# A two-layer decoder step on one core: convolution rows, weight transfers and small loads of the mixer put in another order

## The chip, the cores and the metric

The kernel runs on one core of a Trainium2 chip. TensorE (PE) does the matmuls, VectorE (DVE) and ScalarE (ACT) the elementwise work, GpSimd (POOL) small elementwise work and the issue of some transfers, SyncE (SP) the issue of all others. The metric is the device time of one execution in microseconds; less is better.

## What is computed

Two layers over 288 tokens (256 of a prompt, 8 sequences of 4), 2048 features wide. The mixer, the first half of a layer, is where the change lies:

```python
z = x @ w_in                          # u | cv | cg, 1024 columns each
y5, h_re, h_im = _s5(u, ...)          # 64 groups, complex scan over positions
g5 = gelu(y5)
s5_out = g5 * sigmoid(g5 @ s5_w_glu)
c = cv * sigmoid(cg)
c, new_conv = _causal_dwconv(c, conv_buf, conv_w, conv_b)   # 31 taps, per channel
c = silu(_ln(c, conv_ln_g, conv_ln_b))
x = _ln(ALPHA * x + concatenate([s5_out, c]) @ w_out, ln1_g, ln1_b)
...                                   # up, 3 taps, SwiGLU, down, LayerNorm
x = _ln(ALPHA * x + sigmoid(x @ pe_w_gate) * (p @ pe_w), ln3_g, ln3_b)
```

The output also holds the last scan states and the convolution inputs `new_conv`.

## The kernel before

Activations lie with features on the 128 partitions and the 288 tokens in the free direction. All weights stream once, in 128x128 blocks, eight blocks (512 KB) to a transfer (`wraw`). ScalarE rounds a transfer's tile to a high part (`whi`), VectorE subtracts to get the low part (`wlo`), and a block costs three matmuls of 288 columns (`run`, lines 372 to 378). The first ten transfers of the program are multiplied unsplit (line 368).

Nothing is scheduled by a tool: the program writes every engine's instructions in the order in which Python emits them. `run` walks the blocks of a phase and adds an estimate of TensorE's time to `pe_t`; every second block calls `tick`, which lets background generators emit pieces of other work. Generators wait with `wait(ns)` and `at(ns, fn)` on that account, so its entries (369 ns a block, 640 ns a convolution step) decide beside which block an instruction stands.

A mixer has these phases: `u0` (64 blocks, the first four tiles of u); eight phases `p0` to `p7` of 32 blocks, each giving the 128 channels of one convolution tile, with four phases `v1` to `v4` of 16 blocks between them (the other tiles of u); `g` (64 blocks, the half-GLU's weights); `o` (256 blocks, the output projection).

Two strands run beside these phases:

* **The scan**, eight steps c. TensorE multiplies u into the state (`inject`, tile `bu`, from `ust` and `em`), VectorE scans, and TensorE multiplies back (`project`, tile `y`, from `tm`, `hin` and `om`). `ust`, `tm` and, in layer 1, the parts of `em` and `om` (`sbt`, `sqb`, `scc`) are loaded by SyncE's queue; GpSimd copies into `hin`, makes the tables `stb` for ScalarE's sine and the decay rows `sd`, and stores `u_d`, `k_d` and `y_d` to memory, from where SyncE loads them in another layout. In layer 2 the tiles come ready from memory (`se_d`, `so_d`, `sk_d`, made during layer 1's FFN by `s5_early`).
* **The convolution**, eight tiles j. GpSimd loads the cached rows into `cbuf` (one buffer), VectorE writes the gated values in, GpSimd stores `cbuf` to memory (`cb_d`), loads the taps `cw` (one buffer), loads `cb_d` four times shifted into `stack` (one buffer, 1.1 MB in four transfers) and stores `cbuf` to the output. `conv(j)` then is eight steps of eight matmuls groups on TensorE (lines 1190 and 1193).

`conv(j - 1)` stands behind phase `p{j}`, and `stack(j)` behind that:

```python
self.run(ph[f"p{j}"], self.xs, ev)
if j:
    conv(j - 1)
while "done" not in part:
    self.late.pop(0)[1]()
stack(j)
```

`conv(6)` closes phase `p7`; `conv(7)` stands behind the first 32 blocks of `g`. A LayerNorm (`ln_finish`) is a chain of thirteen short VectorE instructions on 96x3 numbers between matmuls; at the end of layer 1 nothing else is there for TensorE in that time.

Of the kernel before, what the change touches and what calls it, by code (L numbers as in the profile page):

```python
# [65 lines left out]
LOOK = 1  # L66
EARLY_LAG = 7000.0
# [60 lines left out]
class Meter:  # L128
# [27 lines left out]
class Core:  # L156
    def __init__(self, tc, a, ctx):
        self.tc, self.nc, self.a, self.ctx = tc, tc.nc, a, ctx
        self.V = Meter(self, tc.nc.vector)
        self.pe_t = self.pe_l = self.dve_t = 0.0  # L160
# [185 lines left out]
    def run(self, blocks, xs, evac, sums=None, wide=False):  # L346
# [4 lines left out]
        for _, k, m in blocks:  # L351
# [17 lines left out]
            else:  # L369
                xh, xl = xs(k)  # L370
                self.pe_t += 369.0
# [35 lines left out]
    def ln_acc(self, st, v, last=False):  # L407
# [4 lines left out]
        if i == 0:  # L412
            def mean():
                cps = self.ln_banks(st, 1)[0]
                nc.tensor.matmul(cps[:, :TOK], self.ones_1, v, start=True, stop=True)
                st["c"], st["s1"], st["s2"] = self.ln_tile("ln_c"), self.ln_tile("ln_s1"), self.ln_tile("ln_s2")
                nc.scalar.activation(st["c"], cps[:, :TOK], AF.Copy, scale=1.0 / P)
# [31 lines left out]
    def ln_finish(self, st, fill=None, keep=False, subs=()):  # L449
# [26 lines left out]
        def sub(n=1):  # L476
            while subs and n:
# [30 lines left out]
        dg = self.lp.tile([TG, 3, TG], F32, tag="ln_dg", name="ln_dg", bufs=1)  # L508
        V.scalar_tensor_tensor(dg, self.ident[:TG, :TG].rearrange("p (o t) -> p o t", o=1).to_broadcast([TG, 3, TG]),
                               -1.0, y.rearrange("p (z o) -> p z o", o=1).to_broadcast([TG, 3, TG]),  # L510
                               op0=OP.mult, op1=OP.mult)
        fill(1)
        nc.tensor.matmul(b0[:, 8:8 + TOK], self.ones_1[:TG], dg.rearrange("p z t -> p (z t)"),
# [209 lines left out]
    def stack_tile(self, mp):  # L723
# [124 lines left out]
    def s5(self, l, mp):  # L848
# [56 lines left out]

        def load_o(c, eng):
            if early:
                o = mp.tile([P, 4, 2, 4, CIN], F32, name="sqb", tag="sqb", bufs=1)
                eng.dma_start(o, early[c][1])
                return (o,)  # L910
# [19 lines left out]
        def make_o(c, cc, bc=None):  # L930

            if early:
                kd, pk = early[c][2], cc
# [21 lines left out]
            kw = kd.rearrange("(q c) w -> c q w", q=4)  # L955

            def back():
                for s in range(4):
                    nc.sync.dma_start(tm[32 * s:32 * s + 32], kw[:, :, (3 - s) * 32:(3 - s) * 32 + P])
                self.at(LOAD_LAG, lambda: state.update(o=c))  # L960
            self.at(2000.0 if early else BACK_LAG, back)
# [60 lines left out]
        def project(c, us):  # L1022
            y = self.ps.tile([P, 512], F32, tag="one", name="y", bufs=1)
            self.pe_t += 1500.0
            for q in range(4):
                o = y[:, q * NCH:(q + 1) * NCH]
                self.strips(o, tm[:, q], us[:, q], True, False)
# [27 lines left out]
        early = self.early  # L1055
        state = {"i": -1, "p": -1, "e": -1, "o": -1, "y": False, "k": False}
# [64 lines left out]
        nxt = []  # L1121
        G.memset(bs, 0.0)
        G.memset(kp[:, 0:3], 0.0)
        G.memset(H[:, :, :, 0:1], 0.0)
        go0 = load_o(0, nc.gpsimd)
        bt0 = None if early else self.s5_load(l, 0, mp, nc.gpsimd, "b")
# [9 lines left out]
    def mixer(self, l, ph):  # L1136
        nc, a = self.nc, self.a
        V = self.V
        with self.tc.tile_pool(name="mx", bufs=1) as mp:
# [13 lines left out]
            stacks, cbuf = {}, {}  # L1153
# [449 lines left out]
```

## Time and profile before

| | |
|---|---|
| median of three runs | 2781.55 us (2775.46 to 2785.64) |
| the profiled execution | 2775.95 us |
| its span, first to last instruction | 2774.2 us |
| mean granted TensorE clock over the span | 0.985 of full |
| instructions | 57927 |
| bytes moved by DMA | 496.12 MB |

The span is what the trace covers; 1.75 us of the execution lie outside it. The clock is the share of 2.4 GHz that TensorE was granted; it has two levels here, 1.2 and 2.4 GHz, so 0.985 is a mean over stretches at either.

### The profile page before, as it was taken

The page shows a single profiled execution, that of the slowest core. Times are in us where ns is not written, and L with a number is a line of the kernel's source. Part 1 is how long each engine was busy: PE and PEld are TensorE (multiplying, and loading weights), DVE is VectorE, ACT ScalarE, POOL GpSimd, SP SyncE. Part 2 cuts the span into 40 slices and gives each one's busy share as a digit, 9 for nine tenths or more (in the row PEclk, how much of TensorE's full clock was granted, in tenths as well). Part 3 has the DMA queues.
Part 4 walks back from the last instruction along what each step waited for, and adds up shares of the span by engine and source line. Part 5 has one row for each costly group of instructions (what it writes and reads, how often), then busy time and mean ns, then how long its engine had stood idle before and what let it go on. Part 6 is the DMA issues. An engine that isn't in the chain of part 4 may idle for free.

```text
span 2774.2 us, 57927 instructions
## 1 busy us (share of the span) xinstructions
PE 2681.2 (97%) x23696; PEld 2622.5 (95%) x23696; DVE 1814.2 (65%) x3017; ACT 1351.3 (49%) x2224; POOL 299.8 (11%) x912
## 2 busy tenths in 40 slices
PE   8889999999999999999987999999999999999997
PEld 7878999999999999999986989999999999999997
DVE  5875768666577556667776548676546664566686
ACT  3444547553455345546453535465434553455363
POOL 3433001000010000000024410010000000000000
PEclk9999999999999999999998999999999999999998
DMA  7887545456556654554457875445554555455542
GB/s 240 240 234 223 174 155 171 149 174 204 183 183 193 207 172 155 172 174 152 161 184 217 244 219 169 151 160 163 180 168 152 170 182 162 156 172 167 167 153 102
DMA packets 188809, 496.12 MB, mean 179 GB/s; under 512 B 46368, under 2 KB 72240, under 8 KB 188544
## 3 DMA queue, kind: packets, MB, share of 16 engines
q1 hardware_dynamic: 174592, 444.00, 49.9%
q0 software_dynamic: 13952, 48.42, 6.2%
q8 instruction: 186, 3.05, 0.5%
q14 instruction: 79, 0.65, 0.1%
HBM read 467.47 MB, written 24.87 MB: 177 GB/s over the span
## 4 chain that ended last, share of the span: by engine, by line
PE 82%; DMA 8%; DVE 5%; issue 2%; ACT 1%; SPq 1%; POOL 1%; ACTq 0%; DVEq 0%; POOLq 0%
PE acc L372 26%; PE acc L378 24%; PE acc L377 24%; DMA out_dram<-cbuf 2%; PE acc L354 2%; PE acc L374 2%; DVE sw L142 1%; DVE wlo L142 1%; DMA cbuf<-in_convi_dram 1%; PE acc L368 1%; DMA wraw<-in_wts_dram 1%; DMA cb_d<-cbuf 1%; PE acc L1190 1%; DMA scc<-in_s5c_dram 1%; DMA sqb<-q_d 1%
## 5 line engine op out<-in xcount | busy, mean ns | idle before, releaser
L372 PE MATMUL acc<-xh,whi 128*128 128x288 f32 x4656 | 1388.7, 298 | 8.2 <-ACT e L1302 3.1
L377 PE MATMUL acc<-xl,whi 128*128 128x288 f32 x4357 | 1289.1, 296 | 0.4
L378 PE MATMUL acc<-xh,wlo 128*128 128x288 f32 x4357 | 1284.4, 295 | 0.4 <-issue 0.4
L142 DVE TENSOR_TENSOR wlo<-wraw,whi 128x1024 fp32r<-128x1024 f32 x766 | 923.4, 1228 | 47.4 <-ACT whi L198 32.8
L198 ACT ACTIVATE whi<-wraw 128x1024 fp32r<-128x1024 f32 x766 | 791.3, 1050 | 321.5 <-PE acc L377 186.6
L372 PEld LDWEIGHTS acc<-xh,whi 128*128 128x128 f32 x4656 | 876.7, 188 | 14.7 <-ACT e L1302 4.1
L377 PEld LDWEIGHTS acc<-xl,whi 128*128 128x128 f32 x4357 | 821.5, 189 | 3.2 <-DVE xl L142 1.3
L378 PEld LDWEIGHTS acc<-xh,wlo 128*128 128x128 f32 x4357 | 823.5, 189 | 0.9 <-issue 0.9
L372 PE MATMUL acc<-hh,whi 128*128 128x288 f32 x1408 | 416.8, 296 | 0.0
L142 DVE SCALAR_TENSOR_TENSOR fo<-fe,parf,fo 128x304 f32<-128x304 f32 x352 | 188.3, 535 | 332.6 <-ACT fo L1335 326.3
L377 PE MATMUL acc<-hl,whi 128*128 128x288 f32 x1312 | 387.8, 296 | 0.0
L378 PE MATMUL acc<-hh,wlo 128*128 128x288 f32 x1312 | 387.5, 295 | 0.0
L372 PEld LDWEIGHTS acc<-hh,whi 128*128 128x128 f32 x1408 | 264.9, 188 | 0.5
L378 PEld LDWEIGHTS acc<-hh,wlo 128*128 128x128 f32 x1312 | 247.2, 188 | 0.0
L377 PEld LDWEIGHTS acc<-hl,whi 128*128 128x128 f32 x1312 | 246.9, 188 | 0.0
L1331 ACT ACTIVATE fe<-acc 128x256 f32<-128x256 f32 x176 | 67.5, 384 | 299.7 <-PE acc L378 299.6
L1341 POOL COPY fstage<-fe 128x9 f32<-128x9 f32 x176 | 43.6, 248 | 1033.6 <-ACT fe L1332 1016.9
L431 ACT ACTIVATE ln_q<-x 128x288 f32<-128x288 f32 x90 | 40.2, 446 | 220.4 <-DVE x L142 220.4
L1335 ACT ACTIVATE fo<-fe,parf 128x304 f32<-128x304 f32 x176 | 112.9, 642 | 17.3 <-ACT fe L1332 1.1
L1355 ACT ACTIVATE hh<-fth 128x288 fp32r<-128x288 f32 x88 | 39.2, 445 | 164.4 <-DVE fth L142 164.4
L142 DVE TENSOR_TENSOR x<-x,acc 128x288 f32<-128x288 f32 x64 | 29.0, 454 | 131.5 <-PE acc L378 131.4
L142 DVE SCALAR_TENSOR_TENSOR x<-x,acc 128x288 f32<-128x288 f32 x64 | 28.9, 452 | 120.7 <-PE acc L378 120.5
(244 smaller groups left out, 2355.0 us busy)
## 6 DMA issues: line engine op xcount, KB each, us to landing
wraw<-in_wts_dram SPq DMA_DIRECT2D x776, 512.0 KB
stack<-cb_d POOLq DMA_DIRECT2D x56, 282.0 KB, 8.8
cw<-in_convw_dram POOLq DMA_DIRECT2D x16, 512.0 KB, 5.3
cbuf<-in_convi_dram POOLq DMA_DIRECT2D x16, 283.5 KB, 5.2
cb_d<-cbuf POOLq DMA_DIRECT2D x16, 283.5 KB, 3.7
out_dram<-cbuf POOLq DMA_DIRECT2D x16, 283.5 KB, 10.3
sbt<-in_s5b_dram SPq DMA_DIRECT2D x15, 256.0 KB
sqb<-q_d SPq DMA_DIRECT2D x60, 64.0 KB
```

The lines of the kernel that those rows point to most:

```text
L142: return f(out, *args, **kw)
L198: self.nc.scalar.activation(hi, self.raw[s], AF.Copy)
L354: nc.tensor.matmul(out, w, xl, start=False, stop=False)
L372: nc.tensor.matmul(out, w[0], xh, start=first, stop=False)
L374: nc.tensor.matmul(out, w[1], xh, start=False, stop=False)
L377: nc.tensor.matmul(out, w[0], xl, start=False, stop=False)
L378: nc.tensor.matmul(out, w[1], xh, start=False, stop=last)
L431: nc.scalar.activation(st["q"], v, AF.Square)
L1331: nc.scalar.activation(e[:, 2:2 + SEQ], acc[:, :SEQ], AF.Copy)
L1335: nc.scalar.activation(o[:, :w], e[:, 2:EW], AF.Identity, bias=self.prm("ffn_conv_b", m), scale=self.prm("ffn_conv_w2", m))
L1341: nc.gpsimd.tensor_copy(stage[:, z, :, 0], e[:, SEQ:EW:6])
L1355: nc.scalar.activation(hh[i], h, AF.Copy, scale=0.5)
```

## The change

1. **Output of the convolution rows.** `convo` is stored from `cb_d` in memory instead of from `cbuf`.
2. **Stack tiles.** Odd j use a second tile `big`, which later holds `phi` and `plo` (they had tiles of their own). `conv(j - 2)` instead of `conv(j - 1)` stands behind `p{j}`; the taps are loaded by themselves (`taps`), behind the convolution that frees `cw`. `conv(6)` moves into `g`, behind block 20; 12 blocks stand between it and `conv(7)`.
3. **Weight transfers.** The transfer that reuses a `wraw` tile was written into SyncE's queue right behind the subtraction that frees the tile. Now an account of VectorE's time (`dve_c`) says when the subtraction should be done, and the transfer is written 500 ns of `pe_t` behind that, or when the next eight blocks begin.
4. **Two tm tiles** in layer 2 (`pw` is the second); the load stands with that of `sqb`, a step earlier.
5. **GpSimd held at layer 2.** A one-column copy that reads `x32[0]` stands ahead of GpSimd's first work of the layer.
6. **Account.** A block counts 400 ns instead of 369, a convolution step 500 instead of 640. `ones_1` and `ln_dg` go, their room is shared with other tiles.

```diff
@@ stream_lo / next_block / tick
-            self.stream_dma(s + RAW_BUFS)
+            self.freed.append((s + RAW_BUFS, self.dve_c + FREE_LAG))
...
             self.stream_lo(s + ahead)
+            self.stream_dma(s + ahead + RAW_BUFS - 1)
...
+        while self.freed and self.freed[0][1] <= self.pe_t:
+            self.stream_dma(self.freed.pop(0)[0])
@@ Meter
+            cost = 150.0 + (2.1 if name == "tensor_tensor_scan" else 1.05) * n
+            self.core.dve_c = max(self.core.dve_c, self.core.pe_t) + cost
@@ run
-                self.pe_t += 369.0
+                self.pe_t += 400.0
@@ stack_tile
+        if j % 2:
+            return self.big_tile().bitcast(F32).rearrange("p (s w) -> p s w", s=4)
@@ s5
+        def load_t(c, kd):
+            t = tms[c % 2]
...
+        if l:
+            G.tensor_copy(kp[:, 0, 0, 0:1], self.x32[0][:, 0:1])
         G.memset(bs, 0.0)
@@ mixer
+            def taps(j):
+                cws[j] = mp.tile([P, 4, 8, 32], F32, tag="cw", name="cw", bufs=1)
+                nc.gpsimd.dma_start(cws[j], a["convw"][l, j])
...
-                nc.gpsimd.dma_start(a["convo"][l, j], cb)
+                nc.gpsimd.dma_start(a["convo"][l, j], d)
...
-                    self.pe_t += 640.0
+                    self.pe_t += 500.0
...
+                if j > 1:
+                    conv(j - 2)
                 if j:
-                    conv(j - 1)
+                    taps(j - 1)
...
-            self.run(ph["g"][:G_CUT[0]], xs_g, ev_g, sums)
+            self.run(ph["g"][:G_CUT[0] - 12], xs_g, ev_g, sums)
+            conv(CVC - 2)
+            taps(CVC - 1)
+            self.run(ph["g"][G_CUT[0] - 12:G_CUT[0]], xs_g, ev_g, sums)
             self.finish(scan)
             conv(CVC - 1)
```

GpSimd's queue at the first convolution tile of layer 2, before (`h` is the initial state):

```order
L1200 DMA cbuf<-in_convi_dram 128x567
L1221 DMA cb_d<-cbuf 128x567
L1158 DMA cw<-in_convw_dram 128x1024
L1163 DMA stack<-cb_d 32x4x564 x4
L1165 DMA out_dram<-cbuf 128x567
L1200 DMA cbuf<-in_convi_dram 128x567
L1009 COPY hin<-h_16682 128x4x8 x2
```

and the same place after the change:

```order
L1225 DMA cbuf<-in_convi_dram 128x567
L1246 DMA cb_d<-cbuf 128x567
L1188 DMA stack<-cb_d 32x4x564 x4
L1190 DMA out_dram<-cb_d 16x4536
L1225 DMA cbuf<-in_convi_dram 128x567
L1029 COPY hin<-h_16677 128x4x8 x2
```

The taps have left this place (they stand a phase later), and the output's source is memory, in 16 rows of 4536 numbers instead of 128 of 567, so that the second load of `cbuf` no longer has the output's store as a reader of its tile ahead of it.

GpSimd's first work of layer 2, before and after:

```order
L869 DMA h_16682<-in_h_dram 128x512
L1122 MEMSET bsm 128x256
L1123 MEMSET kp 128x96
L1124 MEMSET hin 128x8
L909 DMA sqb<-so_d_7908 128x512
L1086 MEMSET om 128x1024
L969 TENSOR_TENSOR stb<-tix,fint 128x288
```

```order
L881 DMA h_16677<-in_h_dram 128x512
L927 DMA sqb<-so_d_7897 128x512
L1146 COPY kp<-x_0_71 128x1
L1147 MEMSET bsm 128x256
L1148 MEMSET kp 128x96
L1149 MEMSET hin 128x8
L1107 MEMSET om 128x1024
L989 TENSOR_TENSOR stb<-tix,fint 128x288
```

The load of `sqb` has moved up, and all elementwise work stands behind a copy that reads the first tile of layer 1's result.

SyncE's queue in layer 2 from the third load of `ust` on, before and after:

```order
L917 DMA ust<-u_d_17041 32x4x72 x4
L909 DMA sqb<-so_d_8986 128x512
L182 DMA wraw<-in_wts_dram 128x1024
L959 DMA tm<-sk_d_8439 32x4x128 x4
L182 DMA wraw<-in_wts_dram 128x1024 x2
L901 DMA sbt<-se_d_9582 128x512
L917 DMA ust<-u_d_17044 32x4x72 x4
```

```order
L936 DMA ust<-u_d_17041 32x4x72 x4
L927 DMA sqb<-so_d_8870 128x512
L922 DMA tm<-sk_d_8871 32x4x128 x4
L186 DMA wraw<-in_wts_dram 128x1024 x3
L936 DMA ust<-u_d_17044 32x4x72 x4
L927 DMA sqb<-so_d_9431 128x512
L922 DMA pw<-sk_d_9432 32x4x128 x4
```

Behind the third `ust` stood the `tm` of step 1 (`sk_d_8439`), two weight transfers further; now that of step 2 (`sk_d_8871`) stands there, with no weight transfer ahead of it, and steps 1 and 3 load into `pw`.

On TensorE the blocks and their order stay; between them the scan's and the convolution's matmuls move. In layer 2 the first convolution stood 22 blocks behind the first `inject` and now stands 74 blocks and two `project` behind it. Between the last `project` and the convolution's LayerNorm there stood 72 blocks and 2.1 convolutions in layer 1, and 74 blocks and 3 convolutions in layer 2; now there stand 72 blocks and 3 convolutions, and 78 blocks and 4 convolutions.

## Rows read from the trace of the kernel before

**Rows 1.** The page's first part: busy us, share of the span, instructions.

```profile
PE 2681.2 (97%) x23696; PEld 2622.5 (95%) x23696; DVE 1814.2 (65%) x3017; ACT 1351.3 (49%) x2224; POOL 299.8 (11%) x912
```

**Rows 2.** Windows: stretch, length, busy of PE, PEld, DVE, ACT, POOL; clock; DMA share; GB/s.

```profile
60.00:255.00 195.00, 171.58 (x2975) 155.82 (x2976) 147.98 (x256) 82.93 (x159) 80.00 (x149) 0.95 0.83 237
408.00:1380.00 972.00, 969.46 (x7362) 965.19 (x7362) 649.98 (x1059) 493.56 (x811) 53.42 (x269) 1.00 0.54 175
1384.00:1400.00 16.00, 7.21 (x42) 5.75 (x41) 11.32 (x25) 3.99 (x7) 9.03 (x16) 0.64 0.21 66
1440.00:1545.00 105.00, 86.66 (x1612) 78.75 (x1613) 60.45 (x86) 43.79 (x76) 42.79 (x81) 0.90 0.76 222
1545.00:1680.00 135.00, 129.77 (x1806) 119.84 (x1797) 76.89 (x122) 56.34 (x99) 37.45 (x67) 0.97 0.78 229
```

**Rows 3.** Waits of TensorE: who, for what; us in all, times, longest.

```profile
PE lnp L513 <- DVE ln_dg L142: 11.7, 6, 7.6
PE acc L1190 <- DMA stack<-cb_d: 10.5, 5, 5.4
PE bu L392 <- DMA ust<-u_d: 9.8, 3, 5.0
PE y L392 <- DMA tm<-sk_d: 6.7, 1, 6.7
PE bu L392 <- ACT em L928: 6.0, 7, 2.2
PE y L392 <- DMA sqb<-q_d: 5.9, 1, 5.9
```

**Rows 4.** Timeline of TensorE at three of them: start, us, instruction [idle before].

```profile
1394.87 1.33 PE L513 MATMUL lnp<-ln_dg,ones 96*128 96x288 f32 x2 [7.59 <-DVE ln_dg L142]
...
1460.49 1.08 PE L1190 MATMUL acc<-stack,cw 128*32 128x256 f32 x8 [5.37 <-DMA stack<-cb_d]
...
1461.47 1.06 PE L1190 MATMUL acc<-stack,cw 128*32 128x256 f32 x8
...
1522.90 0.47 PE L392 MATMUL y<-ust,tm 128*32 128x72 f32 x8 [6.66 <-DMA tm<-sk_d]
```

**Rows 5.** Timeline of VectorE: first and last instruction of two LayerNorm chains.

```profile
1274.34 0.16 DVE L142 TENSOR_SCALAR ln_ne<-lnp 96x6 f32<-96x6 f32 x1 [2.99 <-PE lnp L462]
...
1277.34 0.46 DVE L142 SCALAR_TENSOR_TENSOR ln_dg<-ident,ln_n 96x288 f32<-96x288 f32 x1
...
1387.32 0.16 DVE L142 TENSOR_SCALAR ln_ne<-lnp 96x6 f32<-96x6 f32 x1 [1.78 <-PE lnp L462]
...
1394.36 0.46 DVE L142 SCALAR_TENSOR_TENSOR ln_dg<-ident,ln_n 96x288 f32<-96x288 f32 x1
```

**Rows 6.** Timeline of VectorE: beside GpSimd (161.60), and behind the LayerNorm of layer 1.

```profile
161.60 0.92 DVE L142 TENSOR_TENSOR yw<-yw,y 128x288 f32<-128x288 f32 x1
...
1412.91 1.22 DVE L142 TENSOR_TENSOR wlo<-wraw,whi 128x1024 fp32r<-128x1024 f32 x1
...
1416.45 1.22 DVE L142 TENSOR_TENSOR wlo<-wraw,whi 128x1024 fp32r<-128x1024 f32 x1
...
1417.95 0.45 DVE L142 TENSOR_TENSOR xl<-x,xh 128x288 fp32r<-128x288 f32 x1
```

**Rows 7.** Waits of GpSimd and of VectorE at cbuf, whole span.

```profile
POOL cbuf L1200 <- DMA out_dram<-cbuf: 90.0, 14, 13.6
...
DVE cbuf L142 <- DMA cbuf<-in_convi_dram: 46.9, 5, 11.3
```

**Rows 8.** Last lines for tile cw and for tile stack, layer 1's mixer: issue to landing.

```profile
DMA to landing us min/median/max: 4.2/5.4/7.5
...
DMA to landing us min/median/max: 5.0/9.2/10.7
```

**Rows 9.** Timeline of TensorE: two steps of an undisturbed convolution.

```profile
80.27 0.64 PE L1190 MATMUL acc<-stack,cw 128*32 128x256 f32 x8
...
80.78 0.62 PE L1190 MATMUL acc<-stack,cw 128*32 128x256 f32 x8
```

More of the change, by code (lines that the diff above doesn't have):

```diff
@@ L66 @@
 LOOK = 1
+FREE_LAG = 500.0
 EARLY_LAG = 7000.0
@@ L414, in mean @@
                 cps = self.ln_banks(st, 1)[0]
[L415 removed]
+                nc.tensor.matmul(cps[:, :TOK], self.ones_d, v, start=True, stop=True)
                 st["c"], st["s1"], st["s2"] = self.ln_tile("ln_c"), self.ln_tile("ln_s1"), self.ln_tile("ln_s2")
[L417 removed]
+                nc.scalar.activation(st["c"], cps[:, :TOK], AF.Copy, scale=float(DM) / P)
                 st["v0"] = v
@@ L721, in until, with big_tile, stack_tile @@
         yield from self.wait(t - self.pe_t)
-    def stack_tile(self, mp):
+    def big_tile(self):
+        return self.pp.tile([P, 4 * STW], F32R, tag="big", name="big", bufs=1)
+    def stack_tile(self, mp, j=0):
+        if j % 2:
+            return self.big_tile().bitcast(F32).rearrange("p (s w) -> p s w", s=4)
         return mp.tile([P, 4, STW], F32, tag="stack", name="stack", bufs=1)
@@ L904, in load_e @@
             return bt, self.s5_load(l, c, mp, eng, "q")
+        def load_t(c, kd):
+            t = tms[c % 2]
+            kw = kd.rearrange("(q c) w -> c q w", q=4)
+            for s in range(4):
+                nc.sync.dma_start(t[32 * s:32 * s + 32], kw[:, :, (3 - s) * 32:(3 - s) * 32 + P])
         def load_o(c, eng):
@@ L909, in load_o @@
                 eng.dma_start(o, early[c][1])
+                load_t(c, early[c][2])
                 return (o,)
@@ L932, in make_o @@
             if early:
-                kd, pk = early[c][2], cc
+                pk = cc
             else:
@@ L954, in make_o @@
                 nc.scalar.activation(of[h, :, :, g], pf[h], AF.Copy)
-            kw = kd.rearrange("(q c) w -> c q w", q=4)
+            if early:
+                self.at(PS_LAG, lambda: state.update(o=c))
+                return
             def back():
-                for s in range(4):
-                    nc.sync.dma_start(tm[32 * s:32 * s + 32], kw[:, :, (3 - s) * 32:(3 - s) * 32 + P])
+                load_t(c, kd)
                 self.at(LOAD_LAG, lambda: state.update(o=c))
-            self.at(2000.0 if early else BACK_LAG, back)
+            self.at(BACK_LAG, back)
         def tables(c):
@@ L1055, in s5 @@
         early = self.early
+        tms = [tm, pw.rearrange("p q i k o -> p (q i k o)")[:, :4 * P].rearrange("p (q m) -> p q m", q=4) if early else tm]
         state = {"i": -1, "p": -1, "e": -1, "o": -1, "y": False, "k": False}
@@ L1121, in s5 @@
         nxt = []
+        go0 = load_o(0, nc.gpsimd)
+        bt0 = None if early else self.s5_load(l, 0, mp, nc.gpsimd, "b")
+        if l:
+            G.tensor_copy(kp[:, 0, 0, 0:1], self.x32[0][:, 0:1])
         G.memset(bs, 0.0)
@@ L1152, in mixer @@
             cst = self.ln_begin(CVC * P)
-            stacks, cbuf = {}, {}
+            stacks, cbuf, cws = {}, {}, {}
+            def taps(j):
+                cws[j] = mp.tile([P, 4, 8, 32], F32, tag="cw", name="cw", bufs=1)
+                nc.gpsimd.dma_start(cws[j], a["convw"][l, j])
             def stack(j):
                 cb, d = cbuf.pop(j)
-                cw = mp.tile([P, 4, 8, 32], F32, tag="cw", name="cw", bufs=1)
-                nc.gpsimd.dma_start(cw, a["convw"][l, j])
-                out = self.stack_tile(mp)
+                out = self.stack_tile(mp, j)
                 def back(eng):
@@ L1164, in stack @@
                 back(nc.gpsimd if j < CVC - 1 else nc.sync)
-                nc.gpsimd.dma_start(a["convo"][l, j], cb)
-                stacks[j] = (out, cw)
+                nc.gpsimd.dma_start(a["convo"][l, j], d)
+                stacks[j] = out
             def window(t, b, off):
@@ L1185, in conv @@
                     self.tick()
-                    self.pe_t += 640.0
-                    if j == CVC - 2 and k >= 4:
+                    self.pe_t += 500.0
+                    if j == CVC - 3 and k >= 4:
                         split_g(n=1)
@@ L1292, in load_p @@
         nc = self.nc
-        self.phi = self.pp.tile([P, PEK, TOK], F32R, name="phi", tag="phi", bufs=1)
-        self.plo = self.pp.tile([P, PEK, TOK], F32R, name="plo", tag="plo", bufs=1)
+        t = self.big_tile()
+        self.phi, self.plo = [t[:, i * PEK * TOK:(i + 1) * PEK * TOK].rearrange("p (k t) -> p k t", k=PEK)
+                              for i in range(2)]
         p32 = mp.tile([P, PEK, TOK], F32, name="p32", tag="sw", bufs=4)
@@ L1435, in build @@
         self.ones_d = pp.tile([P, P], F32, name="ones_d")
-        self.ones_1 = pp.tile([P, P], F32, name="ones_1")
         self.ident = pp.tile([P, P], F32, name="ident")
```

18 lines of the change are left out of this document (8 added, 10 removed).

## The prediction

> **What bounds the kernel now.** I read the page's first part first, then windows by stage, then TensorE's waits, and only then single stretches. TensorE is busy for 97% of the span [rows 1], and the windows show where the rest is: through the FFN of layer 1 it idles 2.5 of 972 us at the full clock, while in the mixers it idles 23.4 of 195 us, 18.3 of 105 and 5.2 of 135, at a clock of 0.95, 0.90 and 0.97, and 8.8 of the 16 us at the end of layer 1, at 0.64 [rows 2]. So only the mixers and that boundary can give anything: about 56 us of idle, and at most 0.05 x 195 + 0.10 x 105 + 0.03 x 135 = 24 us more for matmuls at half clock behind an idle stretch. The block count stays the same, and a block costs 972 / 7362 x 3 = 0.396 us [rows 2]. The other engines are not the limit on average, but VectorE is busy 148 of 195 us in layer 1's mixer [rows 2], which leaves little to catch up with. What ends TensorE's idle time there: the convolution waits 10.5 us for stack loads, inject 9.8 for `ust` and 6.0 for ScalarE's `em`, project 6.7 for `tm` and 5.9 for a load named `sqb`, and the LayerNorm chains 11.7, of which 7.6 at the end of layer 1 [rows 3, 4].
>
> **The change part by part.** The sum is made against the profiled execution, 2775.95 us, which lies 5.6 us below the median of 2781.55 and at the low end of the three runs; I give the result on its scale, and half a dozen microseconds between scales are inside the range.
>
> *GpSimd held at layer 2.* VectorE's LayerNorm chain takes 1394.36 - 1387.32 = 7.04 us there, and the same thirteen instructions take 3.00 us elsewhere [rows 5]. GpSimd is busy 9.0 of 16 us beside it [rows 2]. With GpSimd held, the chain should take 3.0: -4.0 us. The held work then runs beside VectorE's normalisation, which paces the first 64 blocks: 3.54 us from one `wlo` to the next, against 8 x 0.396 = 3.17 for TensorE's eight blocks [rows 2, 6]. A subtraction of 288 columns took 0.92 us beside GpSimd's elementwise work and 0.45 without it [rows 6]. In 9 us there stand some seven instructions of that kind (two `xl` and one `wlo` every 3.54 us): 7 x 0.47 = 3.3 us lost. Net -0.7; bounds -4.0 (no loss behind) to +5.0 (all 9.0 us lost). The Trainium skill ("SBUF — State Buffer", section "SBUF: two separate sides") says that VectorE and GpSimd share one pair of ports under an exclusive lock, and that an instruction of VectorE with two inputs in SBUF waits out a GpSimd instruction that reads SBUF. The row at 161.60 agrees. By that rule the held work costs again where VectorE paces, and in the extreme the term is the +5.0.
>
> *Stack tiles and a later convolution.* All five waits for stack, 10.5 us [rows 3], should go: a stack load lands within 10.7 us in layer 1's mixer [rows 8], and a phase of 32 blocks (12.7 us) now lies between it and its convolution; for layer 2's first tile, 52 more blocks. Behind the longest the convolution ran at half clock, 0.98 us a step against 0.51 [rows 4, 9], for some four steps: -2 more. Bounds -10.5 to -14; I take -12.5. What comes new is the wait for the last taps: `cw` is free only when `conv(6)` ends, and 12 blocks, 4.75 us, cover a load that takes 4.2, 5.4 or 7.5 [rows 8]. That is 0, 0.65 or 2.75 us, twice: +1.3, bounds 0 and +5.5. Behind that wait on GpSimd's queue stands only the last output store.
>
> *Two tm tiles.* The 6.66 us wait for `tm` [rows 4] comes since one tile must be read by a project before SyncE may load the next. With two it is loaded a step earlier: -6.7, and, as an estimate, 1.5 of the 10.5 us that the window's clock of 0.90 is worth [rows 2]. What would be late next there is the step's `sqb` or H, which no row shows; bounds -8.2 and 0, and I take -6, near the row.
>
> *Output from memory.* GpSimd waited 90.0 us, 14 times, for the output's store before it could load the next `cbuf`, and VectorE waited 46.9 us for those loads [rows 7]. These waits go, but not all their time comes back: the `cbuf` load still lies behind four stack loads in GpSimd's queue, which need 9.2 us to land [rows 8], so it lands perhaps 4 us sooner (a longest wait of 13.6 against 9.2), not 13.6. What does come at once is the elementwise work behind the wait: `hin`, tables, and so scan and `em`. Of TensorE's 6.0 us for `em` [rows 3] and the few at half clock behind them I take 4; bounds 0 and -10. The store itself moves the same bytes over the same engines; I cost it at nothing.
>
> *Weights by the account of VectorE.* SyncE's queue is strictly in order, so a weight transfer that waits for a subtraction holds the `ust`, `sqb` and `tm` behind it. What hangs on these loads is 9.8 + 5.9 us [rows 3], and some 10 us at half clock at most (0.05 x 195 of the first window [rows 2]). But in the order of the changed program the two big ones of layer 1, 5.0 and 5.9, still stand right behind the same burst of GpSimd's queue (taps, four stack loads, output store), and a stack load of that burst alone takes up to 10.7 us to land [rows 8]. I take -5; bounds 0 and -25. A weight transfer can be late by at most eight blocks, 3.2 us, since the next eight blocks write it in any case; four tiles stand ahead.
>
> *Less cover.* A convolution is eight steps of 0.51 us [rows 9], 4.0 us. Between the last project and the convolution's LayerNorm there is now 0.875 of one more in layer 1 and one and four blocks more in layer 2: 3.5 + 5.6 = 9.1 us of TensorE's work no longer lie beside the scan. Where the scan is late, that comes as idle time. I take a third, +3; bounds 0 (the scan is early) and +9.1.
>
> The new entries of the account move every lag a little (22 instead of 24 blocks between the first two injects of layer 1); that is in the last term. Sum: -0.7 - 12.5 + 1.3 - 6 - 4 - 5 + 3 = -23.9, so 2775.95 - 23.9 = 2752 us.
>
> **The rivals.** *A, the waits move.* What stands by itself is the stack term and the boundary, -12.5 - 0.7 + 1.3 = -11.9. The rest may only shift: the DMA engines are at a share of 0.83 and 0.76 in the mixers [rows 2], loads land late whoever issues them, and a wait ended early may be followed by the next load's. For it: three of TensorE's waits are for different loads of the same step. Against it: the `tm` wait has a cause of its own, one tile. Time 2764. *B, the bursts dissolve too.* If the early queue takes most of the waits for `ust` and `sqb` with their half clock, another 15 to 20 us go: 2735. For it: in the new order no weight transfer stands between a step's `ust`, `sqb` and `tm`. Against it: the burst's place, as above. *C, the scan is the limit, slower than before.* If the scan's own chain (VectorE at 148 of 195 us [rows 2]) sets the time from first inject to last project, then each wait taken from the convolution comes back at the next inject or project, and the tail behind the last project adds 9.1 us in full: 2785. It decides as soon as VectorE idles no more between the scan's steps. Against it: VectorE still idles 45 of 105 us in layer 2's first half [rows 2]. *D, the held work costs more than it frees:* if VectorE stands still for all of GpSimd's 9.0 us, as the subtraction at 161.60 did for a part of it [rows 2, 6], the boundary term is +5.0 instead of -0.7, and the sum is 2758; the place is the first 64 blocks of layer 2, where VectorE sets the pace. [...]
>
> **How the numbers follow.** The forecast (2745 to 2760) has 0.45, A 0.20, B 0.15, C 0.10, D 0.10. The likeliest gives 2752. The range is 2724 (B with the largest tm and em terms: 2735 - 2 - 6, less 3 of the unmeasured rest of the loads) to 2780 (C short of its full price); I leave 1 in 10 out at each end. A measurement here tells about 0.5%, 14 us, from no change. Faster by more than that, under 2767.6 on the scale of the median, which is about 2762 on the profile's: the forecast, B, most of D and a third of A, 0.72. Within it: the rest of A and D and a part of C, 0.20. Slower by more: C with a stall of its own, 0.08.
>
> **What would show it.** In the changed profile no TensorE wait for stack should be left, the wait for the layer-1 boundary chain should be about 3.5 us instead of 7.6, and GpSimd's wait for the output's store should be gone from its list. A wait of the convolution for `cw` of 0 to 3 us should stand once in each mixer. `tm` should be gone or be replaced by a shorter wait for `sqb` or `ust` in the same project. The clock of the window from inject to the first convolutions of layer 2 should rise from 0.90 to 0.95 or more. I am wrong if inject's waits for `ust` and `em` grow by what the convolution's lose (A or C), or if the first 64 blocks of layer 2 end no sooner behind the boundary than before (D).

## The result and the profile after

The changed kernel takes 2741.94 us (median of 4 runs, 2738.66 to 2748.08) beside 2781.70 (2775.46 to 2785.64): ratio 0.9862, 95% interval 0.9836 to 0.9887. The forecast of 2752 was 10 us too high, inside its range. The profiled execution took 2743.43 us, 32.5 less than the one profiled before. The medians fell by 39.8 us, for the execution profiled before lies 5.7 us below the median of its kernel and the one after 1.5 above; the sum of the prediction was -23.9, so that 9 us are missing on the scale of the profiles and 16 on that of the medians.

The page's first part after, beside [rows 1]:

```profile
PE 2660.2 (97%) x23696; PEld 2600.8 (95%) x23696; DVE 1808.4 (66%) x3016; ACT 1352.9 (49%) x2224; POOL 305.0 (11%) x913
```

TensorE is busy for 21 us less with the same 23696 matmuls, and idle for 81.4 us (span less busy time) instead of 93.0: of the 32.5 us only 11.6 are idle time. Shorter waits alone don't make an engine less busy: either fewer matmuls ran at half clock (the mean clock rose from 0.985 to 0.991), or a matmul has become cheaper at the full one; both come out below. The windows of the same stages (length, then busy time of PE, PEld, DVE, ACT, POOL; clock; DMA share; GB/s), beside [rows 2]:

```profile
60.00:255.00 195.00, 176.73 (x2977) 159.44 (x2977) 147.91 (x259) 88.47 (x166) 81.66 (x152) 0.96 0.89 253
...
1364.00:1380.00 16.00, 11.17 (x76) 9.72 (x75) 9.99 (x30) 4.64 (x10) 2.18 (x7) 0.76 0.37 120
1430.00:1530.00 100.00, 87.93 (x1602) 81.73 (x1601) 64.07 (x88) 49.46 (x86) 47.90 (x93) 0.98 0.85 255
```

In layer 1's mixer TensorE idles 18.3 of 195 us instead of 23.4. At the end of layer 1, a window of the same length about the same chain, the clock is 0.76 instead of 0.64, and GpSimd is busy for 2.2 us there instead of 9.0. In layer 2's first half TensorE still idles 12.1 us of 100 (before 18.3 of 105), and the clock is 0.98 instead of 0.90: many short waits have taken the place of a few long ones, and less of the stretch runs at 1.2 GHz.

TensorE's waits after (who, for what; us in all, times, longest), beside [rows 3]:

```profile
PE lnp L520 <- DVE ln_q L145: 8.1, 6, 3.6
PE bu L399 <- DMA ust<-u_d: 7.8, 4, 3.6
PE acc L375 <- DMA wraw<-in_wts_dram: 7.1, 1, 7.1
PE bu L399 <- ACT em L947: 6.5, 8, 4.0
PE y L399 <- issue: 4.3, 2, 2.8
PE acc L384 <- issue: 3.7, 1, 3.7
PE acc L1215 <- issue: 3.5, 1, 3.5
...
PE y L399 <- POOL hin L1029: 2.9, 1, 2.9
PE acc L1215 <- ACT xh L538: 2.2, 1, 2.2
```

The waits for stack (10.5 us), for layer 2's `tm` (6.7) and for `sqb` (5.9) are gone. The chain at the end of layer 1 costs 3.6 instead of 7.6. The 7.1 us for `wraw` stand at the start of the program and were 5.9 before. What else stands in their place are waits of 2 to 4 us, several of them with no releaser that the profile shows ("issue"). At `cbuf` (waits of all engines, beside [rows 7]) one line of the two is left:

```profile
DVE cbuf L145 <- DMA cbuf<-in_convi_dram: 24.9, 4, 9.1
```

GpSimd's wait of 90.0 us for the output's store has gone; VectorE's for the loads has halved. The wait for the last taps, which the change adds, can be seen in layer 1. The timeline of GpSimd (issue) and of TensorE (the convolution) there:

```profile
264.86 0.56 POOL L1180 DMA_DIRECT2D cw<-in_convw_dram  x1 [7.77 <-PE acc L1218]
```

```profile
273.03 0.86 PE L1215 MATMUL acc<-big,cw 128*32 128x256 f32 x6 [3.53 <-issue]
```

From issue to first use are 8.2 us, and the taps landed 8.1 us behind their issue. At the same place in layer 2 TensorE waits 2.2 us (`PE acc L1215 <- ACT xh` above), 6.9 us behind the issue of the taps; the profile puts that wait down to ScalarE, and when these taps landed isn't recorded, so that it is the taps is likely, not shown.

### The profile page after: what moved, and what is told of

Same layout as the page of the kernel before. It is cut to its first block, busy times and chain, and to the rows that moved or that the text cites. A ratio compares the mean times of both kernels' runs of the same rounds, so it can differ in the third digit from the quotient of the medians.

```text
span 2741.6 us, 57943 instructions
## 1 busy us (share of the span) xinstructions
PE 2660.2 (97%) x23696; PEld 2600.8 (95%) x23696; DVE 1808.4 (66%) x3016; ACT 1352.9 (49%) x2224; POOL 305.0 (11%) x913
## 5 line engine op out<-in xcount | busy, mean ns | idle before, releaser
L145 DVE TENSOR_TENSOR wlo<-wraw,whi 128x1024 fp32r<-128x1024 f32 x766 | 921.3, 1225 | 41.6 <-ACT whi L202 23.9
```

## The experiments

Ratios are to the kernel before, timed on the same chip in the same job (its medians there 2780.6 to 2783.0). Differences to the changed kernel are taken from its 2741.94 us in another job, four runs that spread over 9 us: a difference of 5 us to it is not clear of noise. A run's waits come from one execution, which need not lie at the median.

### The pace of a matmul

The first surprise stands outside the mixers. The window from 1900 to 2200 us, inside layer 2's FFN, where TensorE never idles, before and after:

```profile
1900.00:2200.00 300.00, 300.00 (x2253) 300.00 (x2253) 170.05 (x238) 142.00 (x222) 15.69 (x97) 1.00 0.52 167
```

```profile
1900.00:2200.00 300.00, 300.00 (x2265) 300.00 (x2265) 171.69 (x240) 143.50 (x223) 15.66 (x97) 1.00 0.52 168
```

The same work at the same full clock, yet 2265 matmuls fit where 2253 did: 132.5 against 133.2 ns on average. Two kinds of block are mixed in that mean. The same stretch in two parts, first blocks that multiply `hh` and `hl` (the FFN's inner values), then blocks that multiply `xh` and `xl` (the layer's values), before and after:

```profile
1980.00:2070.00 90.00, 90.00 (x678) 90.00 (x678) 42.92 (x50) 32.42 (x35) 0.87 (x3) 1.00 0.54 178
2080.00:2260.00 180.00, 180.00 (x1353) 180.00 (x1352) 110.43 (x163) 94.84 (x166) 13.21 (x84) 1.00 0.51 163
```

```profile
1950.00:2040.00 90.00, 90.00 (x678) 90.00 (x678) 43.72 (x52) 33.06 (x35) 0.88 (x3) 1.00 0.55 180
2050.00:2230.00 180.00, 180.00 (x1363) 180.00 (x1362) 111.04 (x164) 95.69 (x166) 13.38 (x85) 1.00 0.50 164
```

The first kind keeps its 678 matmuls in 90 us; only the second gains, 1363 for 1353 in 180 us, 0.7%. No edit touches the FFN's matmuls. But since `ones_1` and the tiles of `phi` and `plo` gave up their places and `big` got one, all tiles allocated behind them moved; `wraw`, `whi` and `wlo` start 64 bytes past a multiple of 256 instead of on it.

**e1: the kernel before, with 64 bytes in front of the weight tiles.**

```diff
+        self.pad = pp.tile([P, 16], F32, name="pad")
```

> The kernel before, with one unused tile of 64 bytes a partition, so that all weight tiles start 64 bytes later, as they stand in the changed kernel (64 over a multiple of 256 instead of 0). No instruction moves. Theory 1: the place of the tiles sets the pace of the matmuls in the FFN, 39.67 us per 100 blocks as in the changed kernel instead of 40.00; some 4300 blocks at full pace give 4300 / 100 x 0.33 = 14 us, so about 2768 us, 0.995 of before. Rival: the pace is a chance of the execution or comes from the later weight transfers; then this kernel keeps 40.00 us per 100 blocks and takes the time of before, 2776 to 2786.

Measured: 2771.24 us, ratio 0.9962 (0.9948 to 0.9976): 10.6 us for a tile that nobody reads. The same window:

```profile
1900.00:2200.00 300.00, 300.00 (x2265) 300.00 (x2264) 171.56 (x239) 142.69 (x223) 15.64 (x97) 1.00 0.51 168
```

**e2: the changed kernel, with 192 bytes, so that the tiles are on a multiple of 256 again.**

```diff
+        self.pad = pp.tile([P, 48], F32, name="pad")
```

> The changed kernel with one unused tile of 192 bytes a partition, so that all weight tiles start on a multiple of 256 bytes again, as before the change. No instruction moves. Theory 1: the pace falls back to 40.00 us per 100 blocks, and the time is some 14 us longer than the changed kernel's 2742, about 2756. Rival: pace and time stay, 39.67 and 2742.

Measured: 2750.68 us, ratio 0.9890 (0.9872 to 0.9908), 8.7 us above the changed kernel, and the slow pace is back:

```profile
1900.00:2200.00 300.00, 300.00 (x2253) 300.00 (x2253) 169.89 (x238) 142.57 (x222) 15.71 (x97) 1.00 0.52 167
```

So about 10 of the 40 us come from where the tiles lie. `xh` and `xl` are allocated ahead of everything that changed and stay where they were, and `hh` and `hl`, which moved, gain nothing (the two parts of the stretch hold 677 and 1363 matmuls in e1, 678 and 1353 in e2): of the operands of the blocks that gained, only the weight tiles have moved. Why blocks with `hh` and `hl`, which use the same weight tiles, gain nothing isn't shown.

### The output's store

**e4: the changed kernel, storing from `cbuf` as before.**

```diff
-                nc.gpsimd.dma_start(a["convo"][l, j], d)
+                nc.gpsimd.dma_start(a["convo"][l, j], cb)
```

> The changed kernel with the output of the convolution rows stored from the tile again instead of from memory. Theory (GpSimd's wait for the store held back its elementwise work and the next loads): GpSimd waits some 90 us for the stores again, VectorE's wait for cbuf grows from 25 to about 45 us, and the time is about 4 us longer, 2746. Rival (the store in 16 rows of 18 KB keeps the DMA engines from small loads and from the instruction queue; TensorE's waits without a releaser in the profile, 17 us in the changed kernel against 7 before, come from it): those waits fall back towards 7 us and the time is 5 us or more shorter, about 2737.

Measured: 2764.88 us, ratio 0.9944 (0.9929 to 0.9958), 23 us above the changed kernel; the prediction's term was 4. Its waits (all engines first, then TensorE):

```profile
POOL cbuf L1225 <- DMA out_dram<-cbuf: 106.2, 13, 14.6
...
ACT stb L996 <- POOL stb L990: 38.8, 7, 10.1
...
DVE sw L145 <- POOL fin L1037: 9.1, 1, 9.1
...
PE bu L399 <- ACT em L947: 9.3, 10, 4.4
...
PE y L399 <- POOL hin L1029: 7.2, 4, 3.5
...
PE acc L361 <- DVE xl L145: 6.6, 2, 4.4
...
PE kps L807 <- DVE bsm L145: 5.1, 1, 5.1
...
PE acc L381 <- DVE wlo L145: 4.3, 2, 3.3
```

GpSimd stands at the store, the `stb` and `fin` behind it come late, ScalarE and VectorE wait for these (38.8 and 9.1 us; after the change the first was 17.1), and since their queues are in order too, TensorE's own operands `xl`, `wlo` and `bsm` come late behind them. One such chain: GpSimd's wait ends at 105.49 us, VectorE's 9.1 us for `fin` at 106.45, TensorE's 5.1 us for `bsm` at 110.27. These five waits of TensorE are 32.5 us; after the change `em`, `hin` and `xl` together cost 10.9, and `bsm` and `wlo` nothing that the list shows. But that difference, 21.6, is not the 23: other waits became shorter (`ust` 5.6 instead of 7.8 us, the two at the last taps gone), and TensorE idles 90.9 us in all instead of 81.4. In the two profiles, 23.2 us apart, 9.5 are idle time and 13.7 are busy time, at a mean clock of 0.986 instead of 0.991; the saturated window holds 2265 matmuls here too. So the five waits that grew are for other engines, not for transfers, and more than half of the price is matmuls at the lower clock.

**e9: the kernel before, with that one line changed.**

```diff
-                nc.gpsimd.dma_start(a["convo"][l, j], cb)
+                nc.gpsimd.dma_start(a["convo"][l, j], d)
```

> The kernel before with one line changed: the convolution's output is stored from the copy in memory instead of from cbuf; nothing else moves, and the weight tiles keep their place. Theory 1 (the part works by itself): the store from the tile kept GpSimd's whole queue standing, so taking that wait away gives most of the 23 us that putting it back cost in the changed kernel: 2755 to 2765 beside 2782 before, ratio 0.990 to 0.994, GpSimd's 90.0 us wait gone, shorter waits of TensorE for em and of VectorE for cbuf. Theory 2 (the part only pays beside the others): TensorE's stack, tm and ust waits of before are DMA-bound or come from single tiles, and they stay and absorb what comes early: ratio 0.997 to 1.000. The term of the prediction was 4 us, ratio 0.9986.

Measured: 2775.69 us, ratio 0.9981 (0.9972 to 0.9989): 5 us by itself, the ratio of Theory 2. TensorE's waits in it:

```profile
PE bu L392 <- DMA ust<-u_d: 14.1, 5, 4.9
...
PE y L392 <- DMA tm<-sk_d: 8.3, 2, 8.0
...
PE acc L1190 <- DMA stack<-cb_d: 6.9, 3, 5.3
```

GpSimd no longer waits for the store, and what TensorE waits for is loads: `ust` 14.1 instead of 9.8 us, `tm` 8.3 instead of 6.7 [rows 3], and another 8.5 for layer 1's. The stack waits shrink but stay. The execution profiled took 2781.48 us, the longest of the eleven, so these waits say where time goes, not how much the median has of it.

### The weight queue

**e5: the changed kernel, with each weight transfer written behind its subtraction again.**

```diff
-            self.freed.append((s + RAW_BUFS, self.dve_c + FREE_LAG))
+            self.stream_dma(s + RAW_BUFS)
```

> The changed kernel with each weight transfer issued again right behind the subtraction that frees its tile, as before. Putting the store back cost 23 us in the changed kernel, while the store alone gave 5 us in the kernel before: some other part makes up the rest only together with it. Theory Q (it is the weight queue): 2755 to 2765, with waits of 4 to 6 us for ust, sqb or tm in layer 1's mixer again. Rival S (it is spread over tm, convolution and queue): 2745 to 2750. Rival N (the account of VectorE does nothing here, the prediction's lower bound): within 3 us of 2742.

Measured: 2752.84 us, ratio 0.9901 (0.9885 to 0.9916), 11 us above the changed kernel: between Theory Q and Rival S by the number, with Q's waits. The timeline of SyncE's sequencer in layer 1's mixer, of GpSimd's beside it, and what TensorE then waits for:

```profile
77.87 8.76 SPq L186 DMA_DIRECT2D wraw<-in_wts_dram  x3
86.74 1.79 SPq L936 DMA_DIRECT2D ust<-u_d  x4
```

```profile
86.77 2.21 POOL L1188 DMA_DIRECT2D big<-cb_d  x4 [3.38 <-DMA cb_d<-cbuf]
```

```profile
100.09 0.47 PE L399 MATMUL bu<-ust,em 128*32 128x72 f32 x8 [11.46 <-DMA ust<-u_d]
```

The same place after the change, SyncE's queue and GpSimd's:

```profile
72.79 11.81 SPq L186 DMA_DIRECT2D wraw<-in_wts_dram  x3
84.70 1.99 SPq L936 DMA_DIRECT2D ust<-u_d  x4
```

```profile
88.07 2.21 POOL L1188 DMA_DIRECT2D big<-cb_d  x4 [4.14 <-DMA cb_d<-cbuf]
```

In e5 three weight transfers hold the queue for 8.76 us, the four loads of `ust` come behind them, and TensorE stands for 11.46 us. But in the changed kernel three weight transfers hold it as well, for 11.81 us. What differs at this step is where they end against GpSimd's burst of stack loads: in the changed kernel the loads of `ust` are out 1.4 us ahead of the four, and TensorE uses them 7.6 us later; in e5 they leave together with the four, and TensorE gets them 11.6 us after the last has left. In that mixer (60 to 310 us) the waits of TensorE are these in e5, and the line of `ust` after the change is the last:

```profile
PE bu L399 <- DMA ust<-u_d: 13.1, 2, 11.5
PE y L399 <- DMA sqb<-q_d: 7.8, 1, 7.8
```

```profile
PE bu L399 <- DMA ust<-u_d: 3.6, 2, 2.9
```

**e11: the kernel before with three edits: e1's 64 bytes, e9's store, and the weights by account** (`FREE_LAG`, `dve_c` and `freed` as in the diff of the change).

> The kernel before with three edits: 64 bytes in front of the weight tiles (2771 by itself), the output stored from memory (5 us by itself) and the weights queued by the account of VectorE. If the three are independent and the account is worth little: 2764 to 2768. Theory Q (store and weight queue only pay together): 2748 to 2756, with TensorE's 5 us waits for ust and sqb in layer 1's mixer gone, and the stack waits and the 6.7 us tm wait of layer 2 still there. Under S it is 2760 to 2765.

Measured: 2746.09 us, ratio 0.9877 (0.9861 to 0.9893). Against e1 alone (0.9962) store and queue together are worth 0.9877 / 0.9962 = 0.9915, 24 us. The store alone gave 5; the queue with the change's other parts but without the store (e4) gave 0.9944 / 0.9962, 5 as well. So the two pay far more together than apart, as far as e4 stands for the queue: a kernel with the queue alone was not run. The sequencer of SyncE shows the queue's part, its waits at weight transfers in layer 1's mixer, before, in e9 and in e11:

```profile
SPq L182 <- DVE wlo L142: 102.9, 30, 11.5
```

```profile
SPq L182 <- DVE wlo L142: 110.8, 30, 12.6
```

```profile
SPq L186 <- DVE wlo L145: 72.0, 23, 12.4
```

The same line is 82.1 us after the change, 116.7 in e5 and 86.0 in e4: without the store from memory the queue's waits are shorter too, and pay little. TensorE's waits of e11 show what is left:

```profile
PE acc L1197 <- DMA stack<-cb_d: 11.1, 3, 5.9
...
PE y L399 <- DMA tm<-sk_d: 6.9, 2, 6.4
PE bu L399 <- DMA ust<-u_d: 3.6, 4, 1.3
```

`ust` has fallen from 14.1 in e9 to 3.6 us, `sqb` is no longer in the list. Stack waits of the same size and the `tm` wait of layer 2 are still there, and yet this kernel has 34 of 38 us (0.0123 against 0.0138 of the time before).

### The convolution, the tm tile, the held GpSimd and the account

**e7: one stack tile and the convolutions back in their phases.**

```diff
-                out = self.stack_tile(mp, j)
+                out = self.stack_tile(mp)
...
-                if j > 1:
-                    conv(j - 2)
                 if j:
-                    taps(j - 1)
+                    conv(j - 1)
...
+                taps(j)
                 stack(j)
...
-            self.run(ph["g"][:G_CUT[0] - 12], xs_g, ev_g, sums)
-            conv(CVC - 2)
-            taps(CVC - 1)
-            self.run(ph["g"][G_CUT[0] - 12:G_CUT[0]], xs_g, ev_g, sums)
+            self.run(ph["g"][:G_CUT[0]], xs_g, ev_g, sums)
```

> The changed kernel with one stack tile, each convolution back in the phase that loads its tile, and the sixth convolution back in its phase; the output still stored from memory. The prediction's terms: 12.5 us of stack waits come back and 1.3 of the cw wait and about 3 of less cover go, 8 us slower, 2750, with stack waits of 10 us in all. Rival 1 (with GpSimd's queue no longer stopped by the store, stack loads land in time anyway): stack waits under 4 us, and with the cw waits of 5.8 us gone and the cover back, 2734 to 2740, faster than the changed kernel. Rival 2 (the later convolution also lets the scan run earlier, which was not in the sum): 2758 or more.

Measured: 2747.11 us, ratio 0.9870 (0.9855 to 0.9885), 5 us above the changed kernel, which is not clear of noise; near the prediction's term, but not by its way: no wait for a stack load is among TensorE's. One tile is in time here. The store and the queue alone don't do that, for e11 has both and waits 11.1 us for stack loads; which other part does isn't shown. The waits stand elsewhere, `em` above all:

```profile
PE bu L399 <- ACT em L947: 11.2, 6, 6.5
```

In all TensorE idles 81.3 us, as after the change (81.4); what the profiled execution has more is busy time, and the clock from 1430 to 1530 us is 0.91 instead of 0.98.

**e6: one tm tile, loaded a step earlier.**

```diff
-        tms = [tm, pw.rearrange(...)[:, :4 * P].rearrange(...) if early else tm]
+        tms = [tm, tm]
```

> The changed kernel with one tm tile again, loaded a step earlier than before but into the tile that the last project reads; the rest as changed. The prediction's term: 6 us lost, 2748, with a wait of 5 to 7 us for tm in layer 2's mixer. Rival (the tm wait of before was a late load of the whole queue, which the other parts have cured): within 3 us of 2742, with a tm wait under 3 us. A third way: SyncE's queue now stands at the tm load until the project has read the tile, with the next ust and weights behind it: 2750 to 2760, with new waits for ust or wraw in both mixers.

Measured: 2743.08 us, ratio 0.9861 (0.9848 to 0.9875). The edit doesn't do what it was to: in layer 2 the load for the next step is then written ahead of the project that should read this step's, so the projection is computed from the next step's `tm`. Waits for `tm` come up (6.4 us, the longest 4.8), and the time is that of the changed kernel all the same. As the order is another than the kernel needs, it says little of what the tile is worth.

**e10: one tm tile, loaded where it was before.**

```diff
-                load_t(c, early[c][2])
                 return (o,)
...
-                pk = cc
+                kd, pk = early[c][2], cc
...
-            if early:
-                self.at(PS_LAG, lambda: state.update(o=c))
-                return
...
-            self.at(BACK_LAG, back)
+            self.at(2000.0 if early else BACK_LAG, back)
...
-        tms = [tm, pw.rearrange(...)[:, :4 * P].rearrange(...) if early else tm]
+        tms = [tm, tm]
```

> The changed kernel with one tm tile, loaded where it was before: behind the step's tables, when the last project has read it. The prediction's term: 2748 (6 us), with a wait of 5 to 7 us for tm in layer 2's mixer. Theory T (tm's early place is the partner of the store): 2755 or more, with further waits for tm. Rival (the other parts have cured the late load): within 3 us of 2742, tm waits under 3 us.

Measured: 2747.15 us, ratio 0.9874 (0.9856 to 0.9892), 5 us above the changed kernel, where the term was 6; that is not clear of noise, and the execution profiled was the longest of the four. In the window of layer 2's first half (1430 to 1530 us) TensorE idles 18.5 us at a clock of 0.90, as before the change. But the wait for `tm` is shorter than before, and `em` has grown from 6.5 to 18.6 us; why isn't shown.

```profile
PE bu L399 <- ACT em L946: 18.6, 10, 7.0
...
PE y L399 <- DMA tm<-sk_d: 3.6, 1, 3.6
```

**e3: GpSimd not held at layer 2.**

```diff
-        if l:
-            G.tensor_copy(kp[:, 0, 0, 0:1], self.x32[0][:, 0:1])
```

> The changed kernel without the copy that holds GpSimd at the start of layer 2. Theory (the hold shortens the chain of the LayerNorm by 4 us and costs less than that behind it): TensorE's idle time before the matmul on ln_q at the end of layer 1 goes from 3.6 back to about 7.6 us, and the time is 2 to 5 us longer, about 2745. Rival (what is taken from the chain is lost in the first 64 blocks of layer 2, which VectorE paces): the time stays within 1 us of 2742, the first inject of layer 2 comes equally long after the end of layer 1's last matmul.

Measured: 2741.97 us, ratio 0.9860 (0.9843 to 0.9877), the time of the changed kernel. The boundary does wait again (TensorE's waits in e3):

```profile
PE lnp L520 <- DVE ln_q L145: 11.9, 6, 7.4
```

VectorE in the changed kernel, beside the held work, shows the other side:

```profile
1383.05 0.44 DVE L145 TENSOR_TENSOR x<-x,lnp 128x288 f32<-128x288 f32 x1
...
1386.32 0.83 DVE L145 TENSOR_TENSOR xl<-x,xh 128x288 fp32r<-128x288 f32 x1
```

The subtraction of two tiles in SBUF takes up to 0.83 us instead of 0.45; the one that reads `lnp` from PSUM stays at 0.44. The Trainium skill ("SBUF — State Buffer", section "SBUF: two separate sides") says that an instruction of VectorE with two inputs in SBUF is held up by one of GpSimd's that reads SBUF, and the trace agrees as to which of these grow. What VectorE loses so in the 10 us is only some 1.1 us (seven instructions longer than their 0.45 or 1.22, summed over the timeline). So what the hold brings at the boundary isn't lost beside the held work: the first inject of layer 2 begins 51.4 us behind the first instruction of the LayerNorm's chain, and 54.4 us in e3. That these 3 us don't show in the time isn't explained; they are within the scatter of the runs.

**e8: the two old costs in the account.**

```diff
-                self.pe_t += 400.0
+                self.pe_t += 369.0
...
-                    self.pe_t += 500.0
+                    self.pe_t += 640.0
```

> The changed kernel with the two old costs in the account of TensorE's time (369 and 640 ns instead of 400 and 500), so that lags between scan steps are counted with the old costs. If these numbers matter as little as the prediction said: within 3 us of 2742. If the lag is what removed the two long ust and sqb waits in layer 1's mixer: 2748 or more, with waits of 5 us at those places again.

Measured: 2736.90 us (2735.61 to 2740.70), ratio 0.9842 (0.9829 to 0.9855): 5 us below the changed kernel, the lowest of all. The long waits of layer 1 don't come back (`ust` 2.0 us in all, the longest 1.1). Both expected outcomes are missed. The intervals of e8 and of the changed kernel overlap, so that e8 beats it is likely, not settled; it beats the kernel before by 44 us.

**e12: e8 with 64 bytes more in front of the weight tiles, 128 past a multiple of 256.**

```diff
+        self.pad = pp.tile([P, 16], F32, name="pad")
```

> The changed kernel with the two old costs of the account (2737 by itself) and 64 bytes more in front of the weight tiles, so that they start 128 bytes past a multiple of 256 instead of 64. If a start at a multiple of 256 is the slow one: 2737 again, and 132.2 ns a matmul in the FFN. If 64 bytes is a particular place: 2742 to 2747, 133.3 ns a matmul. In both, the mixers stay as they are with the old costs.

Measured: 2753.11 us, ratio 0.9899 (0.9884 to 0.9914), 16 us above e8, at the slow pace:

```profile
1900.00:2200.00 300.00, 300.00 (x2253) 300.00 (x2252) 170.03 (x238) 142.48 (x222) 15.67 (x97) 1.00 0.52 167
```

Of three places, 0 and 128 are slow and 64 is fast. The pace is worth some 10 of these 16 us, by e1 and e2; the rest isn't explained: in e12's profile an inject in layer 1's mixer waits 6.9 us, put down to a weight transfer, which e8 doesn't have.

## Why the prediction was right, and where it wasn't

The sign, the range and most of the named signs hold, but that the sum comes out near the time is partly luck, for large errors stand in different terms. Store and queue were put at -9 and bring 24 us as a pair (e11), the tiles' place at nothing and brings 10; the other parts were put at -0.7 - 8.2 - 6 = -14.9, and what the changed kernel has beyond e11, the account's costs among it, is 4 us.

* **What bounds the kernel.** "The block count stays the same, and a block costs 972 / 7362 x 3 = 0.396 us" is the step that failed: the sum let TensorE's pace outside the mixers be constant. It fell by 0.5% (0.7% in the blocks with `xh` and `xl`), some 10 us by e1 and e2, which is the larger part of the 16 us by which the medians fell further than the sum. The signs that were named for the mixers could not have shown it; the number of matmuls in a saturated window does.
* **Output from memory, -4.** The step "it lands perhaps 4 us sooner" looked at the loads of `cbuf`, and of the elementwise work behind the store only `em` was counted. With the weight queue as changed, the term is 23 us (e4), through `hin`, `stb` and the in-order queues of ScalarE and VectorE, and through more matmuls at the lower clock; alone it is 5 (e9), near what was said. The bound of -10 was too tight because terms were bounded one at a time.
* **Weights by the account, -5.** That the two big ones of layer 1 "still stand right behind the same burst of GpSimd's queue" is so: in the changed kernel that `ust` leaves at 152.84 us, behind stack loads of 147.86, and that `sqb` at 183.65, beside stack loads of 182.52. But the waits are gone, although the burst is slower than before (tile stack in layer 1's mixer, issue to landing; 10.7 us at most before [rows 8]):

```profile
DMA to landing us min/median/max: 6.9/11.1/14.4
```

  So the burst alone doesn't make these loads late; how early SyncE's queue lets them out decides. With the transfers written at once long waits are there again (e5, 11 us): `sqb` at the same step as before, its loads from 201.57 us on, `ust` at another, where it leaves with the burst. The term is twice what was taken. Rival B, which had 0.15, gave as its reason that "in the new order no weight transfer stands between a step's `ust`, `sqb` and `tm`". That is layer 2's order; in layer 1 two still stand between `ust` and `tm` (at 87.75 us), only they hold the queue for 1.97 us, where three held it for 9.97 before (at 91.66).

* **Stack tiles and later convolution, -12.5 + 1.3 + 3 for cover = -8.2.** Net size near (e7, 5 us, within noise); mechanism only half. All stack waits went, as said, but with the other parts in place one tile has none either, so that the tile is not what removes them there. In e11, where they remain (11.1 us, with the `tm` wait and the boundary's), the time is only 4 us above the changed kernel's. The `cw` wait was 3.5 us and, if the second is one, 2.2, instead of 0.65 twice, the first outside the stated 0 to 3, since the taps took 8.1 us to land and the longest row was 7.5. The +3 for less cover was not measured by itself.
* **Two tm tiles, -6.** Near in size (e10, 5 us, within noise). The clock of that window rose from 0.90 to 0.98, past the 0.95 named, and is 0.90 in e10; but e7, with two tiles, has 0.91, so the clock is not the tile's alone.
* **GpSimd held, -0.7.** The boundary wait fell from 7.6 to 3.6, as said, and nothing is left of it in the time (e3). The working isn't confirmed: VectorE lost about 1.1 us there, not 3.3, and in the two profiles e3's span is 3.2 us longer than that of the changed kernel. That is within the scatter of the runs, so a gain of some 3 us isn't excluded. (The row at 161.60 that gave the price is a product, not a subtraction; it too has two inputs in SBUF, so the reading stands.)
* **The account's costs** had no term of their own. They cost 5 us (e8, likely, not settled); which place isn't found.
* **Rivals.** A, C and D are out: the waits didn't move in full, VectorE's scan isn't the limit (e11 gains 24 us without touching it), and the hold doesn't cost. B came true in part, in layer 1.

By undoing one part at a time the changed kernel loses 23 (store), 11 (queue), 9 (place), 5 (convolution), 5 (tm), 0 (hold) and gains 5 (costs): 48 in all, more than the 40 there are, since store and queue are counted in each other; the fives are within noise.

## What to carry to other kernels

Two queues that are in order and hold each other's consumers are one limit: price the edits to both together, since one alone may show a fifth of the pair (5 of 24 us here). When a wait stands in a queue, follow all that is written behind it to the engines that use it, the elementwise work before the loads. And when an edit changes allocations, compare the count of instructions in a saturated window of both kernels, operand by operand, before you explain the rest by waits. Waits summed from a list are not the time either: set them beside the engine's idle and busy time of the whole span.

## What the runs showed of the hardware that was not expected

Matmuls of 288 columns at the full clock take 133.2 ns or 132.5 ns each on average (2253 or 2265 in 300 us) according to where the tiles behind the pad lie: slow with the weight tiles at 0 (before, e2) and at 128 bytes (e12) past a multiple of 256, fast at 64 (e1, e11 and the changed kernel). The difference is all in blocks with `xh` and `xl` (1353 or 1363 in 180 us); blocks with `hh` and `hl` keep 677 or 678 in 90 us. And the output's store from memory to memory, in 16 rows of 4536 numbers, takes nothing from the mixers that could be seen, though the DMA share in layer 1's mixer rose from 0.83 to 0.89; no run has its price alone. Beside GpSimd's elementwise work VectorE's short instructions with one input grow too: in e3 a TENSOR_SCALAR on 96x3 numbers takes up to 0.60 us, with GpSimd held 0.17. The waits without a releaser, of up to 3.7 us in the changed kernel, remain unexplained but for the 3.5 at the last taps; they stand in e4 too, where the store comes from `cbuf` (11.4 us in all, 17.1 after the change), so its packets are not their main cause.
